# A late accumulator for half of a convolution, and a deferred block of projection columns, in a hybrid encoder layer

## The chip, the cores and the metric

The kernel runs on one core of one Trainium2 chip. The metric is the device time of one execution in microseconds (us). Five engines work side by side, each on its own queue in order: TensorE (PE) multiplies matrices, VectorE (DVE) and ScalarE (ACT) work element by element, GpSimd (POOL) mainly issues gathers here, SyncE (SP) issues transfers.

## The reference

One layer over 256 tokens of width 2048, in float32:

```
hn   = rms_norm(x);  proj = hn @ w_in                       # 2048 -> 3 x 1024: conv_a, conv_gate, ssm_u
yc   = silu(layer_norm(depthwise_conv31(conv_a * sigmoid(conv_gate))))
ys   = z * sigmoid(z @ glu_w),  z = gelu(s5_scan(ssm_u))    # S5: 64 groups x 64 states
h    = x + [rms_norm(yc) | rms_norm(ys)] @ w_out
h    = h + cross_attention(rms_norm(h), rms_norm(mem))      # 256 memory tokens, 4 heads, w_kv: 2048 -> 4096
h    = h + peer(rms_norm(h))                                # top-16 experts of 16384, 8 heads
out  = rms_norm(h)
```

The change lies in the first part: the projections, the S5 recurrence, the convolution and `w_out`.

## The kernel before

**Order of the work.** The program text is one long sequence of instructions, and a planner turns it into one fixed queue for each engine. It simulates the engines: whenever one is free it takes the ready instruction of the lowest priority number, which is its place in the text, lowered by an offset where the text is inside `tc.high_priority(offset=...)`. A weight tile's load, its cast and its low half have the offset `AHEAD` = 500 instructions, an S5 step has `S5_AHEAD` = 700, the convolution has none. On the chip each engine then runs its queue strictly in that order. Tiles that share a tag take the tag's buffers in turn; a new one waits until the one that had its buffer has been read for the last time.

**`linear`** (lines 146 to 187) is every projection. It goes over 512 output columns at a time. For each pair of 128-row blocks of the weight it loads a 512 KB tile (L155, SP), casts it to a high half (L162, ACT), subtracts that for a low half (L163, DVE), and multiplies three times: 24 matmuls of 256 columns (L181 to L183) where the result is channel-major, or 12 of 512 columns (L172 to L174) where it is token-major. Raw tiles have five buffers, high and low halves three each. With `whole` the last pair of blocks goes into the product unsplit (L140, L143), so such a group of 512 columns has seven split tiles and one whole.

**The first part in the order of its text:** the S5 input of `w_in` (2 groups of 512 columns); S5 constants; then twice `conv_a` and `conv_gate` (4 groups), with one S5 step after each group; the memory's norm and transposes; the keys K (4 groups, an S5 step after each); the values V (4 groups); GELU and split of the S5 result; the S5 gate product `ssm_glu_w` (GLU, 2 groups of four tiles); the S5 half's norm; the upper half of `w_out` (rows that belong to S5, 4 groups of four tiles); the convolution; its layer norm, SiLU and group norm; and the lower half of `w_out`, which needs them.

**S5** has eight steps (`s5_body`, L426 to L469), one for each 128 channels: small matmuls into PSUM (L445), products with rotation tables (L446 to L451), eight scans (L456), products back (L459 to L462), matmuls (L466) and the sum into `uT` (L469). The temporaries t1 and t3 share tag `s5c`, one buffer.

**The convolution** (L560 to L568) is 31 taps by eight blocks of 128 channels, 248 DVE instructions of 128x256, each adding one tap to `acc`, an 8 KB tile of its own in pool `mp`. The planner puts them wherever it sees VectorE free. After it come the mean over channels (`chan_sum`, PE L510), the subtraction L571, squares (ACT L517), another channel sum, the root (ACT L523), reciprocal (L524), L573, SiLU (ACT L575), squares, sum, root and reciprocal once more, L531, and the split into yT (L103, L104).

**The activations** memT and yT share buffers by name (`act_tiles`, pool `at`, one buffer each): a yT tile can be written once memT's of that name has been read for the last time.

Of the kernel before, what the change touches and what calls it, by code (L numbers as in the profile page):

```python
# [9 lines left out]
F32 = mybir.dt.float32  # L10
# [10 lines left out]
P = 128  # L21
# [43 lines left out]
SETTLE_RATE = 2.4  # L65
SETTLE_AT = 185
LAG = 2
R_BY = ('AAAA', 'AAVA')


@with_exitstack
def trunk(ctx, tc, a, out, dbg=None):
# [47 lines left out]
    uctx = ctx.enter_context(ExitStack())  # L120
    with ExitStack() as wctx:
        atx = wctx.enter_context(ExitStack())
        wp = wctx.enter_context(tc.tile_pool(name="wp", bufs=3, side="right"))
# [22 lines left out]
        def linear(x, w, c0, ncol, evac, rows_out, kt=KT, korder=None, ahead=AHEAD, whole=None, cols=None):  # L146
            xh, xl = x
            js = korder or range(kt // KG)
            for n, (c, w_) in enumerate(cols or [(c, 512) for c in range(c0, c0 + ncol, 512)]):
                ncb = w_ // P  # L150
                ps = [psm.tile([P, 512] if rows_out else [P, 2, T], F32, name="mm", tag="mm") for _ in range(2)]
                for m, j in enumerate(js):
                    with tc.high_priority(offset=ahead):
                        raw = wp.tile([P, KG, w_], F32, name="w_raw", bufs=5)
                        SY.dma_start(raw, w[j * KG * P:(j + 1) * KG * P, c:c + w_].rearrange("(k p) c -> p k c", p=P))  # L155
# [5 lines left out]
                        lo = wp.tile([P, KG, w_], F32R, name="w_lo")  # L161
                        S.copy(hi, raw)  # L162
                        V.tensor_sub(lo, raw, hi.bitcast(F32))  # L163
# [24 lines left out]
        def run(g):  # L188
            for _ in g:
                pass  # L190
# [5 lines left out]
        with ExitStack() as mctx:  # L196
# [276 lines left out]
            def s5_next():  # L473
                q = s5["q"]
                if q < CQ:
                  with tc.high_priority(offset=S5_AHEAD):
# [2 lines left out]
                    s5_body(q, now)  # L479
                    s5["q"] = q + 1  # L480

            for n in range(2):
                run(linear(xT, a["w_in"], n * 512, 512, ev_a(n), False, whole=xW if W_IN else None))
                s5_next()
                run(linear(xT, a["w_in"], CH + n * 512, 512, ev_g(n), False, whole=xW if W_IN else None))
                s5_next()
# [9 lines left out]
                S.copy(t, ps)  # L496
                SY.dma_start(v_dram[:, tt, 512 * n:512 * n + 512], t)

            for _ in linear(memT, a["w_kv_mem"], 0, D, ev_k, False, whole=memW if W_K else None):
                s5_next()  # L500
            kv_v = linear(memT, a["w_kv_mem"], D, D, ev_v, True, whole=memW if W_V else None)
            run(kv_v)
            for j in range(2):
                z = uT[:, 4 * j:4 * j + 4, :]
                S.activation(z, z, AF.Gelu_apprx_tanh)
# [7 lines left out]
            def squares(src):  # L513
                out = []
                for j in range(2):
                    t = s5w.tile([P, 4, T], F32, name="sqh", tag="s5b")
                    S.activation(t, src[:, 4 * j:4 * j + 4, :], AF.Square)  # L517
                    out.append(t)
                return out

# [6 lines left out]
            def group_norm(src, col, hi, lo):  # L527
                r = chan_rstd(chan_sum(squares(src)))
                for j in range(2):
                    for q in range(4 * j, 4 * j + 4):  # L530
                        V.scalar_tensor_tensor(src[:, q, :], src[:, q, :], colv[:, col, q:q + 1], r, op0=ALU.mult,  # L531
                                               op1=ALU.mult)
                    split(hi[j], lo[j], src[:, 4 * j:4 * j + 4, :])
# [12 lines left out]
            run(linear(zs, a["ssm_glu_w"], 0, CH, ev_glu, False, kt=CQ))  # L546

            yT = act_tiles()
            group_norm(uT, 4, yT[0][2:], yT[1][2:])

            def ev_half(n, tt, ps):
                t = rows.tile([P, 512], F32, name="xh", tag="xc", bufs=2)
# [4 lines left out]

            run(linear(yT, a["w_out"], 0, D, ev_half, True, korder=list(range(4, 8))))

            acc = mp.tile([P, CQ, T], F32, name="acc")  # L560
            for k in range(CW):
                for q in range(CQ):
                    src = cpad[:, q, k:k + T]
                    if k == 0:
                        V.tensor_scalar(acc[:, q, :], src, cwT[:, q, 0:1], colv[:, 0, q:q + 1], op0=ALU.mult,
                                        op1=ALU.add)
                    else:
                        V.scalar_tensor_tensor(acc[:, q, :], src, cwT[:, q, k:k + 1], acc[:, q, :],  # L568
                                               op0=ALU.mult, op1=ALU.add)
# [4 lines left out]
            for q in range(CQ):  # L574
                S.activation(acc[:, q, :], acc[:, q, :], AF.Silu, bias=colv[:, 2, q:q + 1],  # L575
                             scale=colv[:, 1, q:q + 1])
            group_norm(acc, 3, yT[0][:2], yT[1][:2])
# [575 lines left out]
```

## Time and profile before

| | |
|---|---|
| time, median of 3 runs (lowest to highest) | 2125.04 us (2120.92 to 2128.39) |
| the profiled execution: its own time, its span | 2121.98 us, 2120.0 us |
| busy: PE, DVE, ACT, POOL | 1970.8, 1760.7, 1024.5, 736.2 us |
| mean granted TensorE clock | 0.972 |
| the part that the change touches | about 60 to 600 us |

Times in the rows below are from the span's start. "x" is a count of instructions. A PE that is "busy" may be running at half clock: the granted clock of a stretch (1 is 2.4 GHz, a half is 1.2 GHz) stands beside it. In a row of a timeline the bracket at the end is the idle time before the instruction and what ended it.

### The profile page before, as it was taken

To read this page: it belongs to the slowest core of one execution; us is meant where nothing else is said; L and a number is where in the kernel's file an instruction comes from. 1 tells how busy PE (TensorE), PEld (TensorE's weight loads), DVE (VectorE), ACT (ScalarE), POOL (GpSimd) and SP (SyncE) were. 2 spreads that over 40 slices of the span, in tenths; PEclk is the share of its full clock that TensorE was granted. 3 is DMA by queue.
4 is the path that set the end of the run, shared out by engine and by line. 5 is a ranking of instruction groups with operands and counts; after the bars stand their busy time and mean duration, and the time that the engine had idled before them with its cause. 6 is when DMAs were issued, how large, how long until landed. Compare 5 with 4: busy or idle time off the path is not lost.

```text
span 2120.0 us, 32032 instructions
## 1 busy us (share of the span) xinstructions
PE 1970.8 (93%) x11619; PEld 1698.4 (80%) x11619; DVE 1760.7 (83%) x2855; ACT 1024.5 (48%) x1746; POOL 736.2 (35%) x548
## 2 busy tenths in 40 slices
PE   8998798999999999899999999689879999999997
PEld 7987786668799988788888888577667888888886
DVE  5789999987665566999986667998888999899997
ACT  5764544436454454333333333578793444444444
POOL 0000000000000002535446665543218877677772
PEclk9999989999999999999999999899999999999998
DMA  7554454554865476798999999998629999999995
GB/s 246 166 179 154 125 149 130 161 177 139 291 222 193 140 232 221 283 321 319 317 336 402 402 406 391 370 327 275 205 90 318 373 348 337 348 336 340 336 340 187
DMA packets 199390, 563.41 MB, mean 266 GB/s; under 512 B 32050, under 2 KB 40866, under 8 KB 199105
## 3 DMA queue, kind: packets, MB, share of 16 engines
q1 hardware_dynamic: 141888, 318.08, 45.5%
q0 software_dynamic: 57344, 243.30, 30.5%
q8 instruction: 91, 1.49, 0.3%
q14 instruction: 67, 0.54, 0.1%
HBM read 549.38 MB, written 11.93 MB: 265 GB/s over the span
## 4 chain that ended last, share of the span: by engine, by line
PE 48%; DVE 25%; issue 13%; POOL 6%; DMA 5%; ACT 2%; SPq 0%; DVEq 0%; POOLq 0%; ACTq 0%
PE acc L1100 8%; PE acc L1101 8%; PE acc L1099 8%; DVE u L861 6%; POOL u L859 5%; PE mm L183 4%; PE mm L181 4%; PE mm L182 4%; DVE acc L568 3%; DVE w_lo L163 3%; PE mm L174 2%; PE mm L173 2%; PE mm L172 2%; PE y L932 1%; DMA hnT<-ib_dram 1%
## 5 line engine op out<-in xcount | busy, mean ns | idle before, releaser
L861 DVE SCALAR_TENSOR_TENSOR u<-u,hnF 128x1280 f32<-128x1280 f32 x256 | 388.6, 1520 | 86.0 <-DMA u<-in_peer_u,uidx 84.6
L1064 POOL DMA_INDIRECT v<-in_peer_v,vidx x256 | 385.7, 1507 | 178.5 <-DVE accg L1066 68.5
L859 POOL DMA_INDIRECT u<-in_peer_u,uidx x256 | 308.1, 1204 | 328.2 <-DVE u L861 254.0
L162 ACT CAST w_hi<-w_raw 128x1024 fp32r<-128x1024 f32 (+2 forms) x228 | 231.4, 1018 | 289.1 <-PE mm L182 125.7
L901 PE MATMUL sy<-hnT,ut 128*128 128x256 f32 x1536 | 357.0, 385 | 7.9 <-ACT ut L897 7.3
L163 DVE TENSOR_TENSOR w_lo<-w_raw,w_hi 128x1024 fp32r<-128x1024 f32 (+2 forms) x228 | 270.8, 1190 | 111.5 <-ACT w_hi L162 111.3
L901 PEld LDWEIGHTS sy<-hnT,ut 128*128 128x128 f32 x1536 | 287.3, 193 | 48.6 <-ACT ut L897 11.9
L103 ACT CAST vh<-vr 128x1472 fp32r<-128x1472 f32 x128 | 183.2, 1431 | 271.0 <-PE acc L1100 165.8
L1100 PE MATMUL acc<-vh,wl 128*128 128x512 f32 (+1 forms) x768 | 296.7, 386 | 4.4 <-DVE wl L1090 4.3
L183 PE MATMUL mm<-aT_hi,w_lo 128*128 128x256 f32 x960 | 273.2, 293 | 27.2 <-DVE w_lo L163 27.1
L1101 PE MATMUL acc<-vl,wh 128*128 128x512 f32 (+1 forms) x768 | 295.9, 386 | 0.0
L742 POOL TENSOR_TENSOR hnT<-aT_hi,aT_lo 128x1024 f32<-128x1024 f32 (+1 forms) x2 | 3.8, 1908 | 814.5 <-ACT w_hi L162 814.5
L181 PE MATMUL mm<-aT_hi,w_hi 128*128 128x256 f32 x960 | 279.0, 294 | 4.0 <-DVE sg L264 2.3
L1099 PE MATMUL acc<-vh,wh 128*128 128x512 f32 (+1 forms) x768 | 276.5, 385 | 3.2 <-ACT vh L103 2.2
L182 PE MATMUL mm<-aT_lo,w_hi 128*128 128x256 f32 x960 | 276.4, 290 | 0.0
L104 DVE TENSOR_TENSOR vl<-vr,vh 128x1472 fp32r<-128x1472 f32 x128 | 216.5, 1692 | 39.6 <-ACT vh L103 36.9
L1066 DVE SCALAR_TENSOR_TENSOR accg<-v,coef,accg 128x576 f32<-128x576 f32 x256 | 208.7, 815 | 12.0 <-DMA v<-in_peer_v,vidx 7.4
L183 PEld LDWEIGHTS mm<-aT_hi,w_lo 128*128 128x128 f32 x960 | 185.5, 197 | 34.9 <-DVE w_lo L163 31.5
L181 PEld LDWEIGHTS mm<-aT_hi,w_hi 128*128 128x128 f32 x960 | 188.5, 197 | 8.3 <-DVE sg L264 2.9
L182 PEld LDWEIGHTS mm<-aT_lo,w_hi 128*128 128x128 f32 x960 | 189.0, 197 | 1.3 <-issue 0.4
L897 ACT COPY ut<-ut 128x768 f32<-128x768 f32 x128 | 100.4, 801 | 165.8 <-PE ut L895 145.9
L1100 PEld LDWEIGHTS acc<-vh,wl 128*128 128x128 f32 x768 | 145.2, 189 | 35.8 <-DVE wl L1090 5.4
(345 smaller groups left out, 3368.6 us busy)
## 6 DMA issues: line engine op xcount, KB each, us to landing
vr<-in_peer_v SPq DMA_DIRECT2D x128, 736.0 KB
raw<-in_peer_u SPq DMA_DIRECT2D x128, 384.0 KB
w_raw<-in_w_kv_mem SPq DMA_DIRECT2D x64, 512.0 KB
w_raw<-in_w_in SPq DMA_DIRECT2D x48, 512.0 KB
w_raw<-in_w_out SPq DMA_DIRECT2D x32, 512.0 KB
w_raw<-in_w_q_mem SPq DMA_DIRECT2D x32, 512.0 KB
w_raw<-in_w_o_mem SPq DMA_DIRECT2D x32, 512.0 KB
hnT<-ib_dram SPq DMA_DIRECT2D x18, 256.0 KB
```

The lines of the kernel that those rows point to most:

```text
L162: S.copy(hi, raw)
L163: V.tensor_sub(lo, raw, hi.bitcast(F32))
L181: PE.matmul(o, wh, ah, start=first and cb % 2 == 0, stop=False, skip_group_check=True)
L182: PE.matmul(o, wh, al, start=False, stop=False, skip_group_check=True)
L183: PE.matmul(o, wl, ah, start=False, stop=last and end, skip_group_check=True)
L859: G.indirect_dma_start(out=u, out_offset=None, in_=a["peer_u"].rearrange("e (q c) -> (e q) c", c=GU), in_offset=bass.IndirectOffsetOnAxis( ...
L861: V.scalar_tensor_tensor(u, u, 1.0, hnF[:, self.tt, :], op0=ALU.mult, op1=ALU.mult, accum_out=self.act[:, j:j + 1])
L901: PE.matmul(ps[:, b % 2, :], ut[:, k, :], hnT[:, k, :], start=k == 0 and b % 2 == 0, stop=k == KD - 1 and b % 2 == 1, skip_group_check=True)
L1064: G.indirect_dma_start(out=v, out_offset=None, in_=table, in_offset=bass.IndirectOffsetOnAxis(ap=vidx[tt][:, j:j + 1], axis=0))
L1099: PE.matmul(o, wh[:, tt, :], vh[:, cs_], start=b == 0, stop=False)
L1100: PE.matmul(o, wl[:, tt, :], vh[:, cs_], start=False, stop=False)
L1101: PE.matmul(o, wh[:, tt, :], vl[:, cs_], start=False, stop=b == NB - 1)
```

## The change

Four things. `linear` gets named constants for its buffer counts, equal to the counts before, and a second way of making the low half by a transfer, which is off everywhere (`dma_lo=False`), so all low halves stay on VectorE. An S5 step is called once before the first `conv_a` group, so that each of the eight steps stands one place earlier in the text. V's fourth group of 512 columns is put in the text behind the S5 half's norm; V takes its rows in the order 4 to 7, 0 to 3, so that it is through with the two memT tiles that the S5 half of yT wants first. And the convolution accumulates in two tiles of 4 KB: channel blocks 0 to 3 in pool `mp`, blocks 4 to 7 in a tile of tag `s5c`, which becomes free when the last S5 step has read its t3. The layer norm goes over two halves (two instructions of 128x1024 for one of 128x2048 in L571 and L573).

```diff
+RAW_BUFS = 5
+HI_BUFS = 3
+LO_BUFS = 3
...
+            s5_next()
             for n in range(2):
                 run(linear(xT, a["w_in"], n * 512, 512, ev_a(n), False, whole=xW if W_IN else None))
                 s5_next()
...
-            kv_v = linear(memT, a["w_kv_mem"], D, D, ev_v, True, whole=memW if W_V else None)
-            run(kv_v)
+            kv_v = linear(memT, a["w_kv_mem"], D, D, ev_v, True, korder=[4, 5, 6, 7, 0, 1, 2, 3],  whole=memW if W_V else None)
+            for _ in range(3):
+                next(kv_v)
...
-            group_norm(uT, 4, yT[0][2:], yT[1][2:])
+            group_norm([uT[:, :4], uT[:, 4:]], 4, yT[0][2:], yT[1][2:])
+            run(kv_v)
...
-            acc = mp.tile([P, CQ, T], F32, name="acc")
+            accs = [mp.tile([P, 4, T], F32, name="acc"), s5w.tile([P, 4, T], F32, name="acc_late", tag="s5c", bufs=1)]
             for k in range(CW):
                 for q in range(CQ):
-                    src = cpad[:, q, k:k + T]
+                    src, o = cpad[:, q, k:k + T], accs[q // 4][:, q % 4, :]
...
-            mean = chan_sum([acc[:, :4, :], acc[:, 4:, :]])
-            V.tensor_sub(acc, acc, bc(mean[:, None, :], [P, CQ, T]))
-            r = chan_rstd(chan_sum(squares(acc)))
-            V.tensor_mul(acc, acc, bc(r[:, None, :], [P, CQ, T]))
+            mean = chan_sum(accs)
+            for x in accs:
+                V.tensor_sub(x, x, bc(mean[:, None, :], [P, 4, T]))
+            r = chan_rstd(chan_sum(squares(accs)))
+            for j, x in enumerate(accs):
+                V.tensor_mul(x, x, bc(r[:, None, :], [P, 4, T]))
```

## Rows read from the trace of the kernel before

**Rows 1.** The page: busy time, share of the span and instructions of each engine.
```profile
PE 1970.8 (93%) x11619; PEld 1698.4 (80%) x11619; DVE 1760.7 (83%) x2855; ACT 1024.5 (48%) x1746; POOL 736.2 (35%) x548
```

**Rows 2.** Busy time by stretch: us, PE, PEld, DVE, ACT, POOL, clock, DMA.
```profile
316.00:437.00 121.00, 109.06 (x563) 78.72 (x561) 121.00 (x197) 50.21 (x66) 0.00 (x0) 0.94 0.52 153
437.00:468.70 31.70, 30.39 (x179) 22.48 (x176) 31.63 (x46) 11.17 (x12) 0.00 (x0) 1.00 0.58 183
468.70:549.60 80.90, 76.72 (x395) 65.00 (x394) 52.83 (x57) 46.34 (x52) 0.00 (x0) 0.98 0.50 169
```

**Rows 3.** The same stretches, the convolution's L568 alone: us, DVE busy (count).
```profile
0.00:222.00 222.00, 15.89 (x36) 0.97 0.60 182
222.00:316.00 94.00, 34.74 (x82) 0.93 0.47 139
316.00:437.00 121.00, 44.30 (x106) 0.94 0.52 153
437.00:468.70 31.70, 7.05 (x17) 1.00 0.58 183
```

**Rows 4.** The same view, the low halves' L163 alone.
```profile
437.00:468.70 31.70, 10.94 (x9) 1.00 0.58 183
468.70:549.60 80.90, 24.89 (x21) 0.98 0.50 169
```

**Rows 5.** Waits from 80 to 470 us: who for whom, total us, times, longest.
```profile
PEld mm L183 <- DVE w_lo L163: 28.8, 15, 5.6
```

**Rows 6.** Instructions of one line: ns min/median/max, first and last start in us.
```profile
L469 DVE SCALAR_TENSOR_TENSOR uT<-uT,colv,yp x8: 466/472/481, 139.1 to 468.2; 128x256 f32<-128x256 f32 x8
L496 ACT COPY kv_ev<-mm x8: 587/588/589, 372.1 to 459.2; 128x512 f32<-128x512 f32 x8
L597 DVE TENSOR_TENSOR h<-h,mm x16: 677/680/689, 562.3 to 810.9; 128x512 f32<-128x512 f32 x16
```

**Rows 7.** Timeline of ACT near 427 us: the first split of the S5 result.
```profile
427.11 1.05 ACT L103 CAST zh<-uT 128x1024 fp32r<-128x1024 f32 x1 [0.38 <-DVE zr L461]
```

**Rows 8.** Timeline of DVE, 494 to 552 us: the norms after the convolution.
```profile
494.07 2.29 DVE L571 TENSOR_TENSOR acc<-acc,chs 128x2048 f32<-128x2048 f32 x1 [1.96 <-PE chs L510]
496.30 1.75 DVE L524 RECIPROCAL ch_r<-ch_r 128x256 f32<-128x256 f32 x1
...
505.14 2.28 DVE L573 TENSOR_TENSOR acc<-acc,ch_r 128x2048 f32<-128x2048 f32 x1
...
525.13 3.26 DVE L531 SCALAR_TENSOR_TENSOR acc<-acc,colv,ch_r 128x256 f32<-128x256 f32 x8
...
530.64 1.22 DVE L104 TENSOR_TENSOR aT_lo<-acc,aT_hi 128x1024 fp32r<-128x1024 f32 x1
...
550.26 1.39 DVE L555 TENSOR_TENSOR xh<-xh,mm 128x512 f32<-128x512 f32 x2
```

**Rows 9.** Timeline of ACT, 509 to 523 us: the same chain.
```profile
509.89 4.05 ACT L575 ACTIVATE acc<-acc,colv 128x256 f32<-128x256 f32 x8
...
514.79 2.00 ACT L517 ACTIVATE sqh<-acc 128x1024 f32<-128x1024 f32 x2
...
521.54 1.28 ACT L523 ACT_TABLE_LOAD   x1
```

**Rows 10.** Timeline of PE, 512 to 524 us: one channel sum's half.
```profile
516.23 1.89 PE L510 MATMUL chs<-sqh,ones 128*128 128x256 f32 x8
```

**Rows 11.** Timeline of PE, 472 to 477 us: the gate product after a short stop.
```profile
472.17 0.38 PE L182 MATMUL mm<-zl,w_hi 128*128 128x256 f32 x1 [0.76 <-DVE zl L104]
...
473.27 0.42 PE L182 MATMUL mm<-zl,w_hi 128*128 128x256 f32 x1
473.48 0.42 PE L183 MATMUL mm<-zh,w_lo 128*128 128x256 f32 x1
...
476.63 0.28 PE L183 MATMUL mm<-zh,w_lo 128*128 128x256 f32 x1
476.75 0.28 PE L181 MATMUL mm<-zh,w_hi 128*128 128x256 f32 x1
```

More of the change, by code (lines that the diff above doesn't have):

```diff
@@ L122, in trunk @@
         atx = wctx.enter_context(ExitStack())
-        wp = wctx.enter_context(tc.tile_pool(name="wp", bufs=3, side="right"))
+        wp = wctx.enter_context(tc.tile_pool(name="wp", bufs=HI_BUFS, side="right"))
         at = atx.enter_context(tc.tile_pool(name="at", bufs=1))
@@ L144, in whole_matmuls, with linear @@
                                   start=first and cb % 2 == 0, stop=last and cb % 2 == 1, skip_group_check=True)
-        def linear(x, w, c0, ncol, evac, rows_out, kt=KT, korder=None, ahead=AHEAD, whole=None, cols=None):
+        def linear(x, w, c0, ncol, evac, rows_out, kt=KT, korder=None, dma_lo=False, ahead=AHEAD, whole=None, cols=None):
             xh, xl = x
@@ L153, in linear @@
                     with tc.high_priority(offset=ahead):
-                        raw = wp.tile([P, KG, w_], F32, name="w_raw", bufs=5)
-                        SY.dma_start(raw, w[j * KG * P:(j + 1) * KG * P, c:c + w_].rearrange("(k p) c -> p k c", p=P))
+                        raw = wp.tile([P, KG, w_], F32, name="w_raw", bufs=RAW_BUFS)
+                        src = w[j * KG * P:(j + 1) * KG * P, c:c + w_].rearrange("(k p) c -> p k c", p=P)
+                        SY.dma_start(raw, src)
                         full = whole is not None and j >= kt // KG - NWHOLE
@@ L160, in linear @@
                         hi = wp.tile([P, KG, w_], F32R, name="w_hi")
-                        lo = wp.tile([P, KG, w_], F32R, name="w_lo")
+                        lo = wp.tile([P, KG, w_], F32R, name="w_lo", bufs=LO_BUFS)
                         S.copy(hi, raw)
-                        V.tensor_sub(lo, raw, hi.bitcast(F32))
+                        if dma_lo and m % 2:
+                            S.activation(lo, raw, AF.Copy, scale=-1.0)
+                            G.dma_start(lo, src, accum_op=ALU.add)
+                        else:
+                            V.tensor_sub(lo, raw, hi.bitcast(F32))
                     for i in range(KG):
@@ L497, in ev_v @@
                 SY.dma_start(v_dram[:, tt, 512 * n:512 * n + 512], t)
-            for _ in linear(memT, a["w_kv_mem"], 0, D, ev_k, False, whole=memW if W_K else None):
+            for _ in linear(memT, a["w_kv_mem"], 0, D, ev_k, False,  whole=memW if W_K else None):
                 s5_next()
-            kv_v = linear(memT, a["w_kv_mem"], D, D, ev_v, True, whole=memW if W_V else None)
-            run(kv_v)
+            kv_v = linear(memT, a["w_kv_mem"], D, D, ev_v, True, korder=[4, 5, 6, 7, 0, 1, 2, 3],  whole=memW if W_V else None)
+            for _ in range(3):
+                next(kv_v)
             for j in range(2):
@@ L516, in squares @@
                     t = s5w.tile([P, 4, T], F32, name="sqh", tag="s5b")
-                    S.activation(t, src[:, 4 * j:4 * j + 4, :], AF.Square)
+                    S.activation(t, src[j], AF.Square)
                     out.append(t)
@@ L529, in group_norm @@
                 for j in range(2):
-                    for q in range(4 * j, 4 * j + 4):
-                        V.scalar_tensor_tensor(src[:, q, :], src[:, q, :], colv[:, col, q:q + 1], r, op0=ALU.mult,
+                    for q in range(4):
+                        o = src[j][:, q, :]
+                        V.scalar_tensor_tensor(o, o, colv[:, col, 4 * j + q:4 * j + q + 1], r, op0=ALU.mult,
                                                op1=ALU.mult)
-                    split(hi[j], lo[j], src[:, 4 * j:4 * j + 4, :])
+                    split(hi[j], lo[j], src[j])
             zs = ([s5w.tile([P, 4, T], F32R, name="zh", tag="sn") for _ in range(2)],
@@ L558, in trunk @@
             run(linear(yT, a["w_out"], 0, D, ev_half, True, korder=list(range(4, 8))))
-            acc = mp.tile([P, CQ, T], F32, name="acc")
+            accs = [mp.tile([P, 4, T], F32, name="acc"), s5w.tile([P, 4, T], F32, name="acc_late", tag="s5c", bufs=1)]
             for k in range(CW):
                 for q in range(CQ):
-                    src = cpad[:, q, k:k + T]
+                    src, o = cpad[:, q, k:k + T], accs[q // 4][:, q % 4, :]
                     if k == 0:
-                        V.tensor_scalar(acc[:, q, :], src, cwT[:, q, 0:1], colv[:, 0, q:q + 1], op0=ALU.mult,
-                                        op1=ALU.add)
-                    else:
-                        V.scalar_tensor_tensor(acc[:, q, :], src, cwT[:, q, k:k + 1], acc[:, q, :],
-                                               op0=ALU.mult, op1=ALU.add)
-            mean = chan_sum([acc[:, :4, :], acc[:, 4:, :]])
-            V.tensor_sub(acc, acc, bc(mean[:, None, :], [P, CQ, T]))
-            r = chan_rstd(chan_sum(squares(acc)))
-            V.tensor_mul(acc, acc, bc(r[:, None, :], [P, CQ, T]))
[L574 to L577, printed above, removed]
+                        V.tensor_scalar(o, src, cwT[:, q, 0:1], colv[:, 0, q:q + 1], op0=ALU.mult, op1=ALU.add)
+                    else:
+                        V.scalar_tensor_tensor(o, src, cwT[:, q, k:k + 1], o, op0=ALU.mult, op1=ALU.add)
+            mean = chan_sum(accs)
[4 more added lines that the diff above has]
+                V.tensor_mul(x, x, bc(r[:, None, :], [P, 4, T]))
+                for q in range(4):
+                    S.activation(x[:, q, :], x[:, q, :], AF.Silu, bias=colv[:, 2, 4 * j + q:4 * j + q + 1],
+                                 scale=colv[:, 1, 4 * j + q:4 * j + q + 1])
+            group_norm(accs, 3, yT[0][:2], yT[1][:2])
         at2 = wctx.enter_context(tc.tile_pool(name="at2", bufs=1, side="right", reuse_waits="tile"))
```

## The prediction

> **What bounds the kernel now.** I read the page first: PE is busy for 93% of the span and VectorE for 83% [rows 1], so neither alone sets the whole; the stage that is changed has to be looked at by itself. The view of busy time by stretch shows it. From 316 to 437 us VectorE has no idle moment (121.00 of 121), while PE is busy 109.06 at a granted clock of 0.94 [rows 2]. The view of waits names the link: PE's loads alone stood 28.8 us for low halves from VectorE between 80 and 470 us [rows 5]. But a full VectorE is no proof of a bound here, since the convolution is filler. So I took the convolution's line out of the same stretches: it is 44.30 us of those 121 and 7.05 of the next 31.7 [rows 3]. Without it VectorE would need 76.7 us where PE needs 109.06 x 0.94 = 102.5: VectorE bounds that stage only because all of the convolution is squeezed into it. After the last S5 step (its last instruction starts at 468.2 [rows 6], ends at 468.7) the picture turns: to 549.6 us PE is busy 76.72 of 80.9 us and VectorE only 52.83 [rows 2], and no convolution is left [rows 3]. Its norms run beside the upper half of `w_out` (rows 8 to 10 lie between 494 and 532 us), and nothing waits for them: the lower half follows on PE without a gap. I call its start the handover. The upper half's last evacuations start at 550.26 [rows 8] and the lower half's first group ends at 562.3 [rows 6], 11 to 12 us later; the handover lies at 551.
>
> So the question is whether the handover moves. All behind it hangs on yT and PE in the same order as before; I let it shift by the same amount.
>
> **The parts that cost nothing or next to it.** The constants have the old values and the transfer path is off: no instruction changes. L571 and L573 become two instructions each: 2.29 us for 128x2048 against 2 x 1.22 for two of 128x1024 (L104) [rows 8], 0.15 lost, and the squares may start a half, 1.15 us, sooner. Between the two I take 0.
>
> S5 one place ahead: L469 runs eight times from 139.1 to 468.2 [rows 6], 47 us a step on average, while the text places the eighth step right behind K, whose successor V copies out its first group at 372.1 [rows 6], a hundred us before that step really ends. The steps lag behind their places because each is a chain through one buffer of t1 and t3, not because their turn comes late. I take 0 for this edit; at most it is worth one step, 47 us earlier for S5's end (a rival), and at worst its work is taken before low halves that PE wants at the start, some us.
>
> **The upper convolution leaves the stage before S5's end.** Each block has 31 instructions, so a half has 124. By 222 us 36 of L568 and, of the lower blocks, 4 first taps are done [rows 3]; that leaves 84 lower ones, which fill about the 82 places to 316 us. From there to S5's end the convolution has nothing to offer. VectorE's content from 316 to 437 falls from 121 to 76.7; PE's 102.5 then sets the pace: 18.5 us gained (bounds 0, if low halves still come late, and 44.3, if S5 need not wait for PE). From 437 to 468.7 VectorE had 31.63, of which 7.05 were convolution [rows 2, 3] and 10.94 nine low halves [rows 4]; about four of these belonged to V's fourth group and go too: 4 x 10.94/9 = 4.9. That leaves 19.7; with 2 to 3 us of waits 22, 10 us gained. VectorE can run ahead of PE by the three buffers of low halves, which brings S5's end forward by perhaps 4 us more. Sum: S5 ends 33 us earlier, at 436 (bounds 412 and 450).
>
> **V's fourth group moves behind the gate product.** Its eight loads on SP, seven casts on ACT, seven low halves on VectorE, its matmuls, and two copies and two stores all come later. Tiles of one tag go in order of the text: the first split of the S5 result was ready to be made long before and ran at 427.11, as soon as L461 had freed its buffer [rows 7]. So this group's halves stand behind all eight gate tiles, whose last tiles wait for S5; it fills PE after the gate product and not before S5's end. PE's work is not less, only later. V's copies run from 372.1 to 459.2 [rows 6], so a group took (459.2 - 372.1)/3 = 29 us with the waits and the slow clock of that stretch, and 29 x 102.5/121 = 25 without them. The upper half of `w_out` queues behind it on PE, SP and ACT. PE's own path from S5's end: in the old run 80.9 us to 549.6, of which the convolution's channel sums no longer lie here (three of two halves, 1.9 us each [rows 10], 11 us) and idle is 4.2 [rows 2]; plus 25: 91. PE could hand over at 436 + 91 = 527.
>
> **The upper convolution after S5's end.** Here VectorE has the 52.83 us of the old stretch [rows 2], minus the norms of the convolution, which come later: 2.29 + 2 x 1.75 + 2.28 + 3.26 + 2 x 1.22 [rows 8] = 13.8, leaving 39.0; plus seven low halves of V, 7 x 24.89/21 [rows 4] = 8.3; plus 124 taps. One tap is 44.30/106 to 7.05/17 [rows 3] = 0.42 us; 124 of them 52. Sum 99. As filler they take whatever is idle, so VectorE runs full and the last tap ends at 436 + 99 = 535, which is already behind PE's 527. Only then can the mean be formed. The chain from there, with nothing in its way: half a channel sum 1.9; L571 2.3; one square 1.0; half a sum 1.9; root 0.5 (as one SiLU) with table load 1.3; reciprocal 1.75; half of L573 1.15; eight SiLU 4.05; squares 2.0; half a sum 1.9; root and table 1.8; reciprocal 1.75; half of L531 1.6; cast 1.0; low half 1.2 [rows 8 to 10] = 27, and with some twelve hops between engines 30. (From 494.07, the start of L571, to 531.9, the end of the first split, the old run took 38 us, sharing ACT and VectorE with `w_out`; with the sum ahead of it 41. That is the upper bound, 27 the lower.) Handover at 565, 14 us after the old one, and PE stands still for some 38 us where it stood for next to none. What was filler in the shade is now at the end of the path.
>
> **PE's clock after the stop.** In the gate product PE waited 0.76 us until 472.17, and already shortly before. A little later, from 473.27 to 476.63, its matmuls follow each other at 0.21 us, and then at 0.12 again [rows 11]: 3.4 us at the lower of its two levels, 1.2 GHz, 1.5 us lost. The Trainium skill, "TensorE: Matmul & The Clock Gate", section "HAM oscillation — how this bites in real kernels", says that a TensorE kept waiting for data is throttled and begins its next burst cold. By that rule the long stop before the lower half costs about those 1.5 us once more, and the sum would be 15 or 16 us in place of 14; the sum below goes without it.
>
> **Sum.** The profiled execution took 2121.98 us, 3.1 below the median of 2125.04. On its own time: 2122 + 14 = 2136; on the median 2139, inside the 7.5 us by which the three runs differ. I forecast 2136.
>
> **Rivals.**
> *S5 ends early enough (faster).* If S5's end comes before 422, the taps and norms (99 + 30 = 129 us) are through by 551: that is the point from which it decides. For it: VectorE's content alone would allow 468.7 - 44.3 - 7.05 - 4.9 = 412, and if the earlier place in the text really pulls the S5 chain, up to 47 us more. Against it: the 47 us steps, far behind their places, and PE's 102.5 us of work in that stretch. At 412 the handover is at 541, 10 us earlier: 2112. The floor is PE: from 316 to 549.6 its idle time is 12 + 1.3 + 4.2 and the missing clock 0.06 x 109 + 0.02 x 77 = 8 [rows 2], so at most 26 us, 2099. Between the two I give it as 2110.
> *It evens out.* S5's end between 416 and 428, or shorter hops in the norms: handover within 6 us of 551, 2125. For it: every bound above straddles this.
> *The taps wait for PE's work (much slower).* If the planner's own simulation sees little idle VectorE time after S5's end, the taps stand behind the low halves of `w_out`: 527 + 52 + 30 = 609, 58 us later, 2180. Against it: in the old queue it found a place for every tap (all 240 of L568 before S5's end, VectorE without a gap from 316 us on [rows 2, 3]).
>
> **How the numbers follow.** Forecast (slower, its own range 2130 to 2148) 0.50; S5 early enough 0.25; even 0.20; taps late 0.05. About 0.3% (6.4 us) is what a measurement of this kernel can tell from no change. Most of the forecast lies above 2131.4 and a little below: slower 0.53, same 0.22, faster 0.25. For 8 in 10 the range takes in most of the faster case and leaves out its last part and the late taps: 2107 to 2152.
>
> **What would show it.** In the changed profile: L568 absent between about 320 us and S5's end, then dense on VectorE; the last L469 ending near 436 and the last L568 near 535; V's fourth group on PE behind the gate product; a PE gap of 30 us or more ahead of the lower half, in the chain of waits as L571, L524, L573, L575, L531. Wrong if L469 ends before 422, or if PE goes into the lower half without a gap: then the taps were hidden and the time is below 2125.

## The result, and the profile after

The changed kernel takes 2116.23 us (median of 8 runs, 2113.0 to 2118.13) where the kernel before took 2128.47 us on the same chip (8 runs): a ratio of 0.994, 95% interval 0.9925 to 0.9955. It is faster by 0.6%, and I had forecast 0.5% slower (2136 against the median of 2125). The time lies in the prediction's range; the case that came true is its first rival, "S5 ends early enough". The profiled execution took 2117.33 us, its span 2115.3.

The page's busy time hardly differs from [rows 1]; what moved is the order of the work:

```profile
PE 1966.0 (93%) x11619; PEld 1695.5 (80%) x11619; DVE 1758.3 (83%) x2857; ACT 1025.0 (48%) x1746; POOL 750.2 (35%) x548
```

The lines that answer to [rows 6], with the taps of each half added. L477 is the S5 sum (L469 before), L505 V's copy, L579 the taps, L609 the addition to h, which runs for the first time behind the first column group of `w_out`'s lower half. Columns as in [rows 6]:

```profile
L477 DVE SCALAR_TENSOR_TENSOR uT<-uT,colv,yp x8: 476/482/501, 139.7 to 416.5; 128x256 f32<-128x256 f32 x8
L505 ACT COPY kv_ev<-mm x8: 565/580/591, 352.7 to 468.7; 128x512 f32<-128x512 f32 x8
L579 DVE SCALAR_TENSOR_TENSOR acc<-cpad,cwT,acc x120: 475/486/503, 149.9 to 355.8; 128x256 f32<-128x256 f32 x120
L579 DVE SCALAR_TENSOR_TENSOR acc_late<-cpad,cwT,acc_late x120: 406/491/503, 413.8 to 502.6; 128x256 f32<-128x256 f32 x120
L609 DVE TENSOR_TENSOR h<-h,mm x16: 680/681/689, 552.4 to 800.3; 128x512 f32<-128x512 f32 x16
```

S5 ends at 417, not at 468.7 as before nor at 436 as forecast. The 120 later taps of the upper half start 3 us ahead of that end (413.8) and all but 4 or so run behind it, to 503, as forecast. The first addition behind the lower half comes 9.9 us earlier (562.3 to 552.4), the last on that line 10.6 earlier (810.9 to 800.3): the time is won before the handover and kept to the last addition at 800 us. What follows can't be read from these two executions: behind that addition the profiled one of the kernel before took 1309.1 us and this one 1315.0, so that the spans differ by 4.7 us only, where the medians of 8 differ by 12.2. The change doesn't touch that part, and why it varies was not tried.

Busy time by stretch, columns as in [rows 2]; first the changed kernel, then two stretches of the kernel before that stood in no rows yet:

```profile
222.00:316.00 94.00, 90.02 (x725) 80.59 (x727) 94.00 (x146) 52.80 (x76) 0.00 (x0) 0.98 0.54 157
316.00:417.00 101.00, 99.17 (x550) 72.04 (x550) 98.31 (x134) 45.86 (x58) 0.00 (x0) 1.00 0.59 177
417.00:468.70 51.70, 48.05 (x264) 40.57 (x262) 51.70 (x100) 25.95 (x28) 0.00 (x0) 0.97 0.44 133
468.70:549.60 80.90, 64.83 (x264) 51.42 (x264) 60.17 (x89) 32.69 (x38) 0.00 (x0) 0.92 0.69 219
```

```profile
222.00:316.00 94.00, 82.53 (x625) 74.83 (x624) 94.00 (x160) 46.23 (x65) 0.00 (x0) 0.93 0.47 139
316.00:417.00 101.00, 89.74 (x473) 66.70 (x471) 101.00 (x168) 44.10 (x59) 0.00 (x0) 0.95 0.51 151
```

From 222 to 417 us VectorE is full in both kernels (192.3 and 195.0 of 195 us), yet TensorE gets 1275 matmuls done (725 + 550) instead of 1098 (625 + 473). It hadn't been at its limit before; it had waited for VectorE.

The taps alone in the changed kernel, for [rows 3]:

```profile
0.00:222.00 222.00, 16.02 (x36) 0.96 0.60 182
222.00:316.00 94.00, 26.91 (x61) 0.98 0.54 157
316.00:417.00 101.00, 11.70 (x28) 1.00 0.59 177
417.00:468.70 51.70, 29.96 (x72) 0.97 0.44 133
```

And the low halves alone (L171, L163 before), the changed kernel first:

```profile
222.00:316.00 94.00, 25.90 (x22) 0.98 0.54 157
316.00:417.00 101.00, 32.98 (x27) 1.00 0.59 177
```

```profile
222.00:316.00 94.00, 23.21 (x20) 0.93 0.47 139
316.00:417.00 101.00, 26.95 (x23) 0.95 0.51 151
417.00:468.70 51.70, 17.67 (x15) 0.97 0.57 175
```

Now the account of S5's end closes to 2 us. Up to S5's end VectorE spent 15.89 + 34.74 + 44.30 + 7.05 = 102.0 us on taps before [rows 3] and 16.02 + 26.91 + 11.70 = 54.6 now: 47.4 less. The low halves from 222 us to that end fell from 56 to 48, 67.8 to 58.9 us, 8.9 less (an instruction across the border of two stretches is counted in both, so the rows' counts add up to 1 or 2 more). Against that stand 2.7 us in which VectorE idled. 47.4 + 8.9 - 2.7 = 53.6; S5's end moved by 51.7. (The low halves fell as much in acc_late_only below, which leaves V's fourth group where it was.)

The price is where the forecast put it, TensorE's stop ahead of the lower half (timeline of PE; in brackets the idle time and its releaser), with the VectorE end of the chain that makes it wait:

```profile
519.05 1.03 PE L520 MATMUL chs<-sqh,ones 128*128 128x256 f32 x4
529.55 5.38 PE L520 MATMUL chs<-sqh,ones 128*128 128x256 f32 x16 [9.47 <-ACT sqh L527]
540.06 0.80 PE L180 MATMUL mm<-w_hi,aT_hi 128*128 128x512 f32 x1 [5.14 <-ACT aT_hi L106]
```

```profile
502.64 0.48 DVE L579 SCALAR_TENSOR_TENSOR acc_late<-cpad,cwT,acc_late 128x256 f32<-128x256 f32 x1
...
521.47 1.75 DVE L534 RECIPROCAL ch_r<-ch_r 128x256 f32<-128x256 f32 x1
...
535.47 1.75 DVE L534 RECIPROCAL ch_r<-ch_r 128x256 f32<-128x256 f32 x1 [9.86 <-ACT ch_r L533]
```

The last tap is through at 503 and the handover lies at 540: the norms take 37 us and leave TensorE 14.6 us without work, in two pieces of 9.47 and 5.14.

### The profile page after: what moved, and what is told of

It reads as the page before. It is cut to its first block, busy times and chain, and to the rows that moved or that the text cites. A ratio compares the mean times of both kernels' runs of the same rounds, so it can differ in the third digit from the quotient of the medians.

```text
span 2115.3 us, 32017 instructions
## 1 busy us (share of the span) xinstructions
PE 1966.0 (93%) x11619; PEld 1695.5 (80%) x11619; DVE 1758.3 (83%) x2857; ACT 1025.0 (48%) x1746; POOL 750.2 (35%) x548
## 4 chain that ended last, share of the span: by engine, by line
PE 47%; DVE 24%; issue 13%; POOL 6%; DMA 6%; ACT 3%; SPq 0%; DVEq 0%; POOLq 0%; ACTq 0%
PE acc L1112 7%; PE acc L1113 7%; PE acc L1111 7%; DVE u L873 6%; POOL u L871 5%; PE mm L191 4%; PE mm L189 4%; PE mm L190 3%; PE mm L181 3%; PE mm L182 3%; PE mm L180 3%; DVE w_lo L171 3%; DMA v<-in_peer_v,vidx 2%; DVE acc_late L579 2%; PE y L944 1%
## 5 line engine op out<-in xcount | busy, mean ns | idle before, releaser
L1076 POOL DMA_INDIRECT v<-in_peer_v,vidx x256 | 408.7, 1596 | 160.2 <-PE pw L978 61.2
L871 POOL DMA_INDIRECT u<-in_peer_u,uidx x256 | 299.8, 1171 | 343.0 <-DVE u L873 271.3
L171 DVE TENSOR_TENSOR w_lo<-w_raw,w_hi 128x1024 fp32r<-128x1024 f32 (+2 forms) x228 | 271.7, 1195 | 99.5 <-ACT w_hi L166 97.8
```

The source lines that it names most:

```text
L871: G.indirect_dma_start(out=u, out_offset=None, in_=a["peer_u"].rearrange("e (q c) -> (e q) c", c=GU), in_offset=bass.IndirectOffsetOnAxis( ...
L1076: G.indirect_dma_start(out=v, out_offset=None, in_=table, in_offset=bass.IndirectOffsetOnAxis(ap=vidx[tt][:, j:j + 1], axis=0))
```

## The experiments

S5's end is the start of the eighth S5 sum. Each ratio is to the kernel before on the same chip. Those marked "none late" have their taps spread ahead of S5's end. All runs but s5_ahead_only, changed_two_groups and changed_again leave the S5 step ahead out.

| kernel | ratio (95%) | S5's end | last late tap | first h addition |
|---|---|---|---|---|
| before | 1 | 468.2 | none late | 562.3 |
| changed | 0.9940 (0.9925 to 0.9955) | 416.5 | 502.6 | 552.4 |
| s5_ahead_only | 1.0025 (1.0010 to 1.0040) | 469.5 | none late | 567.6 |
| halves_only | 1.0027 (1.0013 to 1.0041) | 467.6 | none late | 565.3 |
| acc_late_only | 0.9951 (0.9925 to 0.9976) | 417.2 | 493.3 | 551.4 |
| v_late_only | 1.0057 (1.0036 to 1.0077) | 460.3 | none late | 576.8 |
| a_v_no_s5_ahead | 0.9943 (0.9923 to 0.9963) | 416.1 | 502.3 | 552.5 |
| a_notaps | 0.9895 (0.9868 to 0.9922) | 418.1 | left out | 537.1 |
| norms_first | 0.9938 (0.9915 to 0.9962) | 414.2 | 500.4 | 549.4 |
| taps_norms_first | 0.9944 (0.9925 to 0.9962) | 416.1 | 501.1 | 551.9 |
| kv_two_products | one run, 2107.84 us | 411.7 | 494.8 | 546.8 |
| v_fills_norms | 0.9934 (0.9912 to 0.9956) | 418.6 | 494.8 | 551.2 |
| v_fills_norms_first | 0.9949 (0.9933 to 0.9966) | 418.8 | 495.1 | 552.4 |
| v_fills_no_late_taps | 1.0085 (1.0058 to 1.0112) | 461.8 | none late | 582.8 |
| two_groups_late | 0.9913 (0.9879 to 0.9947) | 408.7 | 486.4 | 549.9 |
| fills_both_norms | 0.9963 (0.9948 to 0.9979) | 407.8 | 494.6 | 552.3 |
| three_groups_late | 1.0003 (0.9991 to 1.0014) | 397.1 | 473.9 | 560.7 |
| changed_two_groups | 0.9906 (0.9890 to 0.9922) | 405.6 | 483.3 | 546.8 |
| changed_again | 0.9948 (0.9934 to 0.9962) | 415.7 | 501.8 | 551.4 |

**Which part does it.** Each part alone, and the taps and V's group together.

a_v_no_s5_ahead, the change without the step ahead:
```diff
-            s5_next()
             for n in range(2):
```


> The changed kernel without the S5 step ahead of its place (the upper taps late, V's fourth group behind the gate product). Theory TAPS (S5 ended 20 us sooner than forecast because the upper taps are gone from the planner's queue between the S5 instructions, and the step's place does nothing): the last S5 step starts at 417 +-4 us, as in the changed kernel, and the time is within 0.2% of the changed kernel's 2116. Rival AHEAD (the earlier place pulled the S5 chain): the last step starts at 430 or later and the time is 2128 or more.

s5_ahead_only: that line alone, V and the accumulator's place as before, the accumulator in two tiles.

> The kernel before with the S5 step ahead alone (two accumulator halves, both in their own place). TAPS: the eight steps stand where they stood, last start 468 +-4, time within 0.3% of before. AHEAD: the last step starts before 458 and the time is 10 us or more below before.

acc_late_only: the upper tile in S5's buffer, V as before.

> The kernel before with the upper taps in the late tile alone; V stays ahead of the gate product. TAPS: the last S5 step starts between 417 and 430, the taps are dense behind it, and PE has a gap before the lower half of w_out; with V's fourth group ahead of the gate product PE has less to do behind S5's end, so the gap is 10 to 20 us longer than the 20 us of the changed kernel, and the time is 0 to 10 us above the changed kernel's (2116 to 2126). Rival VLATE (S5 ends sooner because V's fourth group no longer stands in its queue): the last step starts at 436 or later, and the time is above before, 2130 or more.

v_late_only: V's fourth group late, both tiles of the accumulator in pool `mp`:
```diff
-... s5w.tile([P, 4, T], F32, name="acc_late", tag="s5c", bufs=1)]
+... mp.tile([P, 4, T], F32, name="acc_late")]
```


> The kernel before with V's fourth group behind the gate product alone; all taps may be placed anywhere, as before. TAPS: the last S5 step starts at 455 to 468 (at most the low halves of V's group are gone), PE stands still for 10 to 20 us before the gate product's second half, the time is 0 to 10 us above before (2128 to 2138). VLATE: the last step starts before 450 and the time is 5 us or more below before.

halves_only: two tiles and the instructions in halves; nothing moved.

> The kernel before with nothing but the accumulator in two tiles of 4 KB, both in their own place, and the two instructions where there was one in the subtraction and the product of the layer norm. s5_ahead_only was 0.25% slower than before and its S5 steps had not moved. Theory HALVES: that loss belongs to the two tiles (their norms come out of the planner in another order): here too 0.1 to 0.4% slower, first group of the lower half near 567 us as there. Rival STEP: the loss belongs to the step ahead: here within 0.1% of before, first group at 562.

The step ahead is worth nothing (0.9943 without it; s5_ahead_only ends S5 at 469.5, and with halves_only's 1.0027 as its base its 1.0025 is no effect). V's group alone costs: v_late_only lies 0.3% above halves_only, with the first h addition 11.5 us later, although S5's end comes 7.3 us earlier. The late taps alone give the whole gain, 0.9951, 0.76% under halves_only (I had expected acc_late_only 0 to 10 us above the changed kernel); V's group beside them changes nothing that can be measured.

Why V's group does so little there shows in V's copies of acc_late_only:

```profile
L504 ACT COPY kv_ev<-mm x8: 564/587/589, 350.9 to 433.3; 128x512 f32<-128x512 f32 x8
```

V stands in the text ahead of the gate product as before, but its fourth group is copied out at 430.8 and 433.3, behind S5's end at 417.2; in the kernel before, all of V came out ahead of it (459.2 against 468.2). With the taps gone the S5 steps overtake V in the queues. Up to 417 us VectorE makes as many low halves in acc_late_only as in a_v_no_s5_ahead (L171 of each, in this order), so moving the group takes none out of that stretch:

```profile
0.00:417.00 417.00, 117.49 (x97) 0.99 0.56 175
0.00:417.00 417.00, 118.01 (x97) 0.98 0.56 175
```

V's group alone fails because VectorE still carries all taps ahead of S5's end, and TensorE has little left to do while it waits for S5. The stretch 437 to 468.7 of v_late_only:

```profile
437.00:468.70 31.70, 17.29 (x98) 12.85 (x98) 23.84 (x38) 5.47 (x5) 0.00 (x0) 0.61 0.14 45
```

TensorE is busy 17.29 of 31.7 us at a clock of 0.61, where the kernel before had 30.39 at 1.00 [rows 2].

The prediction gave the halves no cost; halves_only costs 0.27%. VectorE's busy time is no longer (1758.7 us, 1760.7 before), but TensorE waits for the S5 half's norm: for its low half, where it stood 0.3 us in the kernel before, and for its high half, where it didn't wait (waits of PE, 468 to 521 us, halves_only):

```profile
PE mm L182 <- DVE aT_lo L107: 2.1, 1, 2.1
PE mm L180 <- ACT aT_hi L106: 1.6, 1, 1.6
```

That the order of the queues, planned anew, does this is argued from these waits; it was not tried by itself.

**What the late taps cost.** a_notaps is acc_late_only without them:
```diff
+                    if k and q >= 4:
+                        continue
                     src, o = cpad[:, q, k:k + T], accs[q // 4][:, q % 4, :]
```


> acc_late_only with 120 of the 124 upper taps left out (the upper blocks get their first tap alone, so the output is not the layer's). Theory TAPS: S5 ends at 417 +-5 as in acc_late_only, so with the taps gone at the end as well only PE is left: the 5 us gap ahead of the lower half goes, the gap in the gate product's tail (about 13 us at 460 to 480) stays or shrinks, time 4 to 15 us below acc_late_only's 2112.8 (2098 to 2109). Rival PACE (S5 ends at 417 because of the order of S5 and V in the queues, and VectorE's time does not matter): time within 3 us of acc_late_only.

2102.13 us against 2112.78, on two chips on which the kernel before took the same to 0.3 us: 10.7 us, and 14.3 us at the first h addition (the rougher figure, since its profiled execution was the longest of its four, 2108.28 us). So the forecast's harm is real: taps at the end cost more than nothing. S5's end stays (418.1). Their harm at the end is smaller than what their absence gives ahead of S5.

**Whether the order in the queues could shorten the end.** norms_first puts the two norms 1200 places ahead; taps_norms_first the upper taps 800 ahead too:
```diff
+            with tc.high_priority(offset=1200):
+                mean = chan_sum(accs)
+                ...
```


> a_v_no_s5_ahead with the norms behind the convolution at an offset of 1200 instructions, so that the planner takes them as soon as they are ready and not behind the upper half of w_out. Theory CHAIN (handover = last tap + norms): the last tap stays at 502, the norms shrink from 38 to about 30 us, PE enters the lower half at 531 to 535 instead of 540, time 5 to 9 us below the changed kernel: ratio to before 0.990 to 0.992. Rival: the norms are bare already, or what they displace costs as much: ratio 0.994.

> As norms_first, and the upper taps at an offset of 800. CHAIN: the taps go ahead of low halves that PE wants only later, the last tap lies at 480 to 492, the norms run beside the upper half of w_out, PE enters the lower half at 518 to 526, ratio to before 0.985 to 0.989. Rival LOWHALF: PE now waits for the low halves of V's fourth group and of w_out, and the ratio stays at 0.992 or above.

Neither differs from a_v_no_s5_ahead: CHAIN was wrong both times. VectorE is full from 417 to 500 us either way, and the chain from the last tap to the handover stays 36 to 38 us (500.8 to 536.7 and 501.6 to 539.1).

**What sets S5's end.** kv_two_products takes a third of TensorE's matmuls on K's and V's split tiles away and leaves VectorE's low halves (the line for token-major results; the one for channel-major is alike):
```diff
-                                PE.matmul(o, al[:, ts], hi[:, i, :], start=False, stop=last)
+                                if not two: PE.matmul(o, al[:, ts], hi[:, i, :], start=False, stop=last)
```


> The changed kernel without its extra S5 step, and K and V made of two products each in place of three (the one with the input's low half is left out, so that the output isn't the layer's); nothing else is edited, and VectorE keeps its subtractions. It takes some 90 us of TensorE between 140 and 420 us down to about 60. Theory PE-PACE (the forecast's: what is left of S5 from 316 us on waits for TensorE's matmuls in the order of its queue): the eighth S5 sum comes at 380 to 395 us rather than 416. Theory VECTOR-PACE (S5 overtakes V in the queues and is held by VectorE's own work): the eighth sum stays within 410 to 418 us and TensorE merely idles more.

```profile
L477 DVE SCALAR_TENSOR_TENSOR uT<-uT,colv,yp x8: 468/474/484, 137.1 to 411.7; 128x256 f32<-128x256 f32 x8
```

```profile
316.00:417.00 101.00, 79.47 (x413) 52.15 (x411) 101.00 (x143) 46.86 (x57) 0.00 (x0) 0.89 0.57 178
```

TensorE now idles 21.5 us of 101 and S5's end comes 4.4 us earlier than in a_v_no_s5_ahead, not 21 to 36 as PE-PACE wanted. TensorE's work isn't what S5 waits for; VectorE is full. (One execution; its time is not used.)

v_fills_norms asks the opposite question, whether V's group may go behind the upper half of `w_out`, into the norms' stop:
```diff
-            run(kv_v)
...
             run(linear(yT, a["w_out"], 0, D, ev_half, True, korder=list(range(4, 8))))
+            run(kv_v)
```


> The changed kernel without its extra S5 step, with V's fourth column group put behind the upper half of w_out instead of ahead of it (the group-normed upper half then lies in the buffers of the S5 gate product, and the group reads its rows in the ordinary order). Theory FILL: the 23 us of TensorE for that group and the 8 subtractions of some 1.1 us on VectorE come to lie in the convolution's norms, where TensorE idles 38 us; the last tap comes 4 to 8 us earlier, the three channel sums run at the full clock (1.9 us rather than 5.4), the first h addition comes at 535 to 545 us rather than 552.5 and the time is 2098 to 2106 us. Theory CHAIN (the handover hangs on the last tap and the chain of norms alone, and the queues put the group where the planner thinks TensorE idle): first h addition within 550 to 556, time 2109 to 2116. Theory LATE (the channel sums now queue behind V's matmuls on TensorE): handover 5 to 15 us later, time 2118 to 2128.

> v_fills_norms with the convolution's two norms put 1200 places ahead in the order of the queues. Theory FILL: if the channel sums queue behind V's matmuls in v_fills_norms, this takes 5 to 10 us off it and comes to 2095 to 2103 us. Theory CHAIN: within 0.15% of v_fills_norms.

> v_fills_norms with both halves of the convolution in one place as before (no late taps). Theory TAPS (the late taps are what makes S5 end early): S5's eighth sum at 455 to 470 us, and the time 2120 to 2135 us, no faster than the kernel before. Theory FILL-ALONE (V's group moved far enough back does it without the late taps): eighth sum at 435 to 455 and the time below 2115 us.

In v_fills_norms the stop is filled and nothing is won (three stretches of its profile):

```profile
440.00:468.70 28.70, 14.73 (x54) 11.18 (x53) 28.40 (x61) 8.07 (x9) 0.00 (x0) 0.64 0.16 55
468.70:521.00 52.30, 52.30 (x231) 43.05 (x230) 44.68 (x66) 20.88 (x21) 0.00 (x0) 1.00 0.70 232
521.00:541.00 20.00, 20.00 (x82) 15.12 (x81) 13.50 (x18) 16.10 (x22) 0.00 (x0) 1.00 0.46 138
```

TensorE is full from 468.7 on, the last tap comes 7.5 us earlier, but 14 us of idle stand at 440 to 468.7 instead, where V's group lay before and TensorE now waits for the S5 half's norm. A hole was moved, not closed: FILL was right on the taps (494.8) and wrong on the time, which is the one that CHAIN gave; and the stop to be filled was never the 38 us that I had put there, but 14.6. The norms 1200 places ahead of that won nothing. Without the late taps the same edit ends S5 at 461.8 and is slower than before by 0.85%, more than TAPS gave it: again the taps make S5 early, not V's place.

**Taking more off VectorE ahead of S5's end.** If VectorE's sum sets that end, seven more low halves out of it must bring it forward:
```diff
-            for _ in range(3):
+            for _ in range(2):
                 next(kv_v)
```


> The changed kernel without its extra S5 step and with V's last two column groups, not the last one alone, behind the S5 gate product. Seven low halves of about 1.15 us each leave the stretch ahead of S5's end. Theory VECTOR-TOTAL: the eighth S5 sum comes 6 to 11 us earlier, at 405 to 411 us; behind it the low halves and 23 us of TensorE come back in front of the upper half of w_out, so that the last tap ends near 500 as before, TensorE's path grows and the time is 2112 to 2124 us. Theory STEP-CHAIN (a step of S5 is held by its own chain, VectorE having other things to fill in): the sum stays within 414 to 418 and the time is 2122 to 2132 us.

> v_fills_norms with V's third column group moved too: it stands behind the first norm (that of the S5 half), the fourth behind the upper half of w_out as there. In v_fills_norms TensorE idled 14 of the 28.7 us from 440 to 468.7 and was full from there to 550. Theory VECTOR-TOTAL: S5's end comes 6 to 11 us earlier (408 to 412 rather than 418.6), the third group fills the gap of the first norm, TensorE goes into the lower half 5 to 10 us earlier, the first h addition is at 541 to 546 us rather than 551.2 and the time 2102 to 2108 us. Theory FULL (behind S5's end TensorE and VectorE together have no room left): the first h addition comes within 549 to 560 and the time is 2110 to 2122 us, whatever S5's end does.

> two_groups_late with a third of V's four column groups behind the S5 gate product. Theory VECTOR-TOTAL: the eighth S5 sum comes 6 to 9 us earlier still, at 400 to 403 us; but behind it TensorE has 23 us more to do in front of the upper half of w_out, and where it had 14.9 us without work between 316 and 417 us in two_groups_late it has some 35. It was full from 414 to 541 us there, so that the handover moves by 23 less 8, some 15 us later, and the time is 2112 to 2122 us. Theory STEP-CHAIN (with this much gone the steps are held by their own chain): the sum stays within 406 to 410 and the time is 2120 to 2130 us.

> The changed kernel with V's last two column groups, not the last one, behind the S5 gate product; its S5 step ahead stays in, which was worth nothing elsewhere. If two_groups_late really is the better kernel: 2100 to 2107 us, ratio to the kernel before 0.989 to 0.9925, and 0.2 to 0.5% below the changed kernel beside it. If its low figure was chance: within 0.15% of the changed kernel.

> The changed kernel itself, beside the one above on the same chip: 2112 to 2118 us, ratio 0.9925 to 0.9955.

Each further group moved brings S5's end 7 to 12 us forward (416.1, 408.7, 397.1 in the runs without the step ahead; 415.7 and 405.6 on one chip with it): the seven halves' 8 us or somewhat more, as VECTOR-TOTAL said, and no sign of STEP-CHAIN. (With three groups I had 400 to 403.) Both times were not as I expected: 2102.9 us for two groups, below 2112 to 2124, and 2125.6 for three, above 2112 to 2122. With two groups late the kernel is faster than with one or three, 0.9906 beside the changed kernel's 0.9948 on the same chip, intervals apart. Of the 8.5 us between these two medians the profiled executions show 4.6 at the first h addition and 5.7 at the last; where the rest comes from is open. I had given two_groups_late 2112 to 2124 us because I took TensorE's path behind S5's end for the limit. The profile of changed_two_groups, three stretches:

```profile
316.00:417.00 101.00, 86.44 (x483) 65.17 (x483) 101.00 (x153) 41.07 (x52) 0.00 (x0) 0.90 0.44 141
...
468.70:521.00 52.30, 52.30 (x227) 42.43 (x226) 38.01 (x51) 27.53 (x33) 0.00 (x0) 1.00 0.65 217
521.00:541.00 20.00, 20.00 (x88) 16.21 (x87) 16.70 (x21) 10.06 (x10) 0.00 (x0) 1.00 0.70 231
```

The changed kernel beside it had TensorE busy 7.16 of those last 20 us, at a clock of 0.69. Here the last tap is through at 483.8, the norms run beside the upper half of `w_out`, and TensorE goes into the lower half without a stop: the third group, which now stands ahead of it too, has pushed the upper half back into what was the hole. With three groups late the taps are done at 474, but now TensorE is the limit (the same view of three_groups_late):

```profile
316.00:417.00 101.00, 73.27 (x458) 56.24 (x457) 100.77 (x161) 38.79 (x48) 0.00 (x0) 0.81 0.31 102
...
521.00:541.00 20.00, 20.00 (x89) 16.33 (x88) 17.03 (x22) 10.48 (x11) 0.00 (x0) 1.00 0.65 212
```

It stands idle 27.7 of the 101 us before 417 and pays for them afterwards: first h addition at 560.7, ratio 1.0003. fills_both_norms ends S5 at 407.8 but puts the fourth group behind `w_out` and stays at 0.9963, as FULL said.

## Why the prediction was wrong

**The failed step: the pace ahead of S5's end.** "PE's 102.5 then sets the pace" gave 436. The bound that I had worked out beside it, VectorE's own content alone, gave 412; S5's end came at 417, ahead of the 422 that I had named as the sign of being wrong. What set it was VectorE's sum and not TensorE's work. The eight sums show where the forecast lost it (the fourth, sixth and seventh, before and changed):

```profile
289.91 0.47 DVE L469 SCALAR_TENSOR_TENSOR uT<-uT,colv,yp 128x256 f32<-128x256 f32 x1
...
389.15 0.47 DVE L469 SCALAR_TENSOR_TENSOR uT<-uT,colv,yp 128x256 f32<-128x256 f32 x1
...
437.63 0.47 DVE L469 SCALAR_TENSOR_TENSOR uT<-uT,colv,yp 128x256 f32<-128x256 f32 x1
```

```profile
277.42 0.48 DVE L477 SCALAR_TENSOR_TENSOR uT<-uT,colv,yp 128x256 f32<-128x256 f32 x1
...
357.31 0.50 DVE L477 SCALAR_TENSOR_TENSOR uT<-uT,colv,yp 128x256 f32<-128x256 f32 x1
...
388.52 0.50 DVE L477 SCALAR_TENSOR_TENSOR uT<-uT,colv,yp 128x256 f32<-128x256 f32 x1
```

By the seventh sum S5 was 49.1 us ahead, where the forecast had 18.5 and some 4 for the buffers; from there to the eighth it gained 2.6 more, where I had 10. Two assumptions failed together. The 102.5 us were TensorE's busy time in a stretch in which it waited for VectorE; how much of its work had to lie there depended on VectorE as well. Once VectorE had 8 us less taps between 222 and 316, TensorE did 100 matmuls more there and came to 316 with less to do. And I had let lower taps fill "about the 82 places to 316": 61 were taken, and S5 was 12.5 us ahead by the fourth sum, before the stretch in which I looked for a gain. kv_two_products shows that TensorE isn't the pace; two_groups_late and three_groups_late show, by 7 to 12 us for each group of halves, that VectorE's sum is. That the bound of 412 was met to 5 us is partly luck: it took off 51.4 us of taps and 4.9 of low halves, and measured were 47.4 and 8.9, less 2.7 of idle.

**S5 one place ahead: right.** Worth nothing, shown twice.

**V's fourth group: right in place, nothing in worth.** It fills TensorE behind the gate product (copies to 468.7) and leaves the time as it is when the taps are late. Alone it is a loss, which I had not priced.

**The taps behind S5's end: right in kind, 13 us too large.** I gave VectorE 99 us to the last tap; it took 86 (417 to 503). All late taps but 4 or so ran there, 48.9 us where I had 52; the other 10 are low halves and additions of `w_out` that I had put ahead of the last tap and that came behind it.

**The norms: 30 us given, 37 measured**, inside the bounds of 27 and 41. I had each channel sum end 1.9 us behind its last input. The second one ended 7.0 us behind it (513.04 to 520.08), with matmuls of `w_out` between its own, and the third 4.5 us (530.44 to 534.93), on a slow TensorE. TensorE's stop was 14.6 us and not some 38: it came to the end of the upper half at 520, 103 us behind S5's end where I had 91, with the first two channel sums among its work there. The two misses behind S5's end partly cancel (86 + 37 = 123 against 99 + 30 = 129), so that S5's end decides: with the forecast's 436 the measured 123 us would still have put the handover at 559, 8 us late; with 417 it lay at 540 instead of 551. The rival with S5's end at 412 gave the handover 541 and 2110 to 2112 us; that it met the handover to 1 us is luck, since its S5 end was 5 us too early and its 129 us 6 too long.

**TensorE's clock: right, and dearer.** After 9.47 us of waiting 16 channel matmuls took 5.38 us, against 1.03 for four at 519.05, some 1.7 us lost (16 took 3.72 in the kernel before); behind the second stop matmuls followed each other at 0.42 us until 542.8, with a granted clock of 0.50, then at 0.235, another 1.2 us. That is 2.9 us, 1.7 of them within the norms' 37, where I had 1.5 outside the sum. The Trainium skill, "TensorE: Matmul & The Clock Gate", section "HAM oscillation — how this bites in real kernels", says that a TensorE which is starved between bursts is throttled and begins the next burst cold; the trace agrees, with that 0.50 behind 5.14 us of waiting:

```profile
540.06:542.79 2.73, 2.73 (x6) 2.06 (x7) 2.73 (x4) 1.04 (x1) 0.00 (x0) 0.50 0.00 0
```

**The halves: wrong.** "Between the two I take 0" was 0.27%, 0.13 to 0.41. The durations, 0.15 us, didn't price the edit; that a split instruction makes two entries in a planned order is my explanation, not shown.

**The chances.** I gave the case that came true 0.25 because the S5 steps stood far behind their places at 47 us each. But that lag was VectorE's full queue itself: with the taps out of it the last five steps came 28 to 43 us apart, where they had come 31 to 52 apart. It was the best argument for the rival and not against it. S5's end at 417 also meets the condition of "It evens out" (416 to 428), but the handover moved 11 us and not up to 6.

## What to carry to other kernels

Here one engine had no idle moment over a stretch, and moving work out of it moved the end of that stretch by nearly the work's whole duration, filler or not; another engine, about 90% busy in the same stretch, was no second limit, because it was waiting for the first. Look for this case, and test it as kv_two_products does. Weigh that against what the moved work costs where it goes, and count both engines' holes on both sides of the point that is moved: of the kernels tried here the best had two groups late, where the chain behind VectorE's last tap was through (531 us) just before TensorE came to the handover, one step past the change and one short of where TensorE starved ahead of S5's end. A hole that is filled by moving work out of another place is not closed.

## What the runs showed of the hardware beyond this

VectorE's instructions aren't recorded with the same length from run to run: the S5 sum took 482 ns (median) in the profiled execution of the changed kernel, 472 in changed_again, which is the same program, and 462 in changed_two_groups; the late taps 491, 476 and 467. But the time from S5's end to the last late tap, over which VectorE is full, was 86.1 us in both executions of the changed kernel (416.5 to 502.6, 415.7 to 501.8). So a longer record wasn't a later end here, and durations of single instructions should be compared between runs with care. What sets them was not tried.
